# Expert rows by indirect DMA and transposes in place of one-hot products, in a mixture of experts on one Trainium2 core

## The chip, the cores and the metric

The kernel runs on one core of one Trainium2 chip. The time is device microseconds of one execution, from three timed runs; a profiled execution of its own gives the trace. Engines: PE is TensorE's matmuls and PEld its weight loads, DVE is VectorE, ACT is ScalarE, POOL is GpSimd, SP is SyncE, whose queue issues the loads of the weights. A q behind an engine's name (SPq, ACTq) is its sequencer, which issues DMAs.

## The reference, cut to what matters

Two blocks are computed on 512 tokens of width 1024 in float32: a first block (a long convolution and a differential attention) and a second one (sparse attention and a mixture of experts). The change touches the mixture of experts alone:

```python
def hier_moe(h, ...):                       # h: rmsnorm(x) * gain, 512 x 1024
    g_sel = argmax(h @ w_group + b_group)   # one of 4 groups
    top_val, top_idx = top_k(e_logit[g_sel], 2)          # 2 of its 8 experts
    weight = softmax(g_logit)[g_sel] * softmax(top_val)
    # for each of 32 experts, on the rows of its tokens:
    gate, up = split(xb @ w_gate_up[e], 2)               # 1024 -> 2 x 256
    y = (silu(gate) * up) @ w_down[e]                    # 256 -> 1024
    # y * weight is summed into the rows of the tokens
x = x + hier_moe(...); out = rmsnorm(x, norm_final)
```

## The kernel before

All of it is traced into one program for the five engines and then ordered by the framework's own scheduler, which keeps each engine's queue in order; a queue waits at its first instruction that isn't ready.

`moe()` begins while the last projection of the mixer runs. For each of the eight blocks m of 128 columns, `after()` adds up the routing logits `lg`, transposes the block `hn` (columns by tokens) to tokens by columns in PSUM (`tp`), and splits it into a high part `Xh` and a low part `Xl`, both 128 x 4 x 1024, so that two fast matmuls with them keep float32 precision. Then comes the routing, for the 4 x 128 tokens at once: GpSimd raises the mean squares to the power -0.5 (`power`, L1832), VectorE does some 30 small operations one after another (two `first_max` for the best and second expert, weights, ranks) and TensorE a few tiny matmuls. The result is `rk` (the place of each token among those of each expert, up to 64 places per expert), `Wd` (weights) and `wr` (six columns per pair of experts: the weights of the two experts and the token's normaliser, each as a high and a low part). At the end of this stage GpSimd adds `acc = Xh + Xl` (L1902), the array of tokens into which the experts' results are added; `issue_after` puts these four additions behind `power` in GpSimd's queue.

The experts' stage works on 16 pairs of experts j, in 8 groups g of two pairs. `gather(g)` makes a 0/1 matrix `P` (tokens by 4 x 64 places) on VectorE and multiplies `Xh` and `Xl` with it (L1923): for each of eight column blocks kk eight matmuls of 256 columns, an eviction to `Xs` (L1929 on VectorE or L1931 on ScalarE, scaled by the norm's gain). That yields the tokens of four experts, columns by places. After kk = 3 it multiplies `wr` with `P` too (L1937), for the weights `sw` and normalisers `sr` of the places. `gate_up(j)` multiplies `Xs` with the streamed weights of two experts, each on a half of TensorE's columns (L1961), `act(j)` transposes the result (L1970) and applies the gate, `down(j)` multiplies with the second weights (L1984), and `combine(g)` brings the results of two pairs back to the tokens with the matrices `PT` (L2002) and adds them to `acc` (L2005). The loop over j at the end of the stage interleaves these: gate_up(j), down(j-1), then steps of `gather(g+1)` and `combine(g-1)`, then act(j).

The weights, 6 MiB per pair, come in jobs of 1 MiB on SP's queue (`_load`, L220 and L229) into nine buffers taken in turn; a load waits until the matmuls that used its buffer are done. Only in case an expert has more than 64 tokens does `overflow()` do more work behind the end.

Of the kernel before, what the change touches and what calls it, by code (L numbers as in the profile page):

```python
# [20 lines left out]
D = 1024  # L21
KD = D // 128
SEQ = 512
# [6 lines left out]
F32 = np.float32  # L30
# [12 lines left out]
def host_consts():  # L43
    c = {}
    c["ident"] = np.eye(128, dtype=F32)

    t = np.linspace(0.0, 1.0, T, dtype=F32)
    w = (F32(2.0 * math.pi) * np.arange(T, dtype=F32) / F32(T)).astype(F32)
# [3 lines left out]
    n = T // 2 + 1  # L52
# [46 lines left out]
    cm = np.zeros((5, 128, 2, 5, 128), F32)  # L99
# [17 lines left out]
    G = np.zeros((5, 128, 2, 266))  # L117
# [16 lines left out]
    p = np.arange(128) % 64  # L134
    j = (p // 32) * 16 + p % 16
# [6 lines left out]
    pi = np.arange(128)  # L142
# [6 lines left out]
    m = np.zeros((128, 64 + 1 + 128 + 8), F32)  # L149
    m[:, 0:64] = np.arange(64)  # L150
    m[:, 64] = pi % 64
    m[:, 65:193] = pi[:, None] < pi[None, :]
    m[:, 193:201] = pi[:, None] + 128 * np.arange(8)[None, :]
    c["moe"] = m
    return c

# [188 lines left out]
N_PAIR = N_EXP // 2  # L345
# [982 lines left out]
def block2_mixer(k, A, C, out, pp, ppc):  # L1328
    nc, tc = k.nc, k.tc
    RC = slice(META, T)  # L1330
    with ExitStack() as ctx:
# [406 lines left out]
        for m in range(KD):  # L1738
# [11 lines left out]
            ml.append(l)  # L1750
        spc.close()
        moe(k, A, C, out, ctx, mhp, Pairs(mh), Pairs(ml))


def moe(k, A, C, out, ctx, mhp, mh, ml):
    nc, tc = k.nc, k.tc
    rt = ctx.enter_context(tc.tile_pool(name="moer", bufs=1, reuse_waits="tile"))
    acc = rt.tile([128, 4, D], FT, name="acc")
    Xh, Xl = (x.rearrange("p a b -> p (a b)")[:, 0:4 * D].rearrange("p (t d) -> p t d", t=4) for x in (k.xh, k.xl))
    cm = rt.tile([128, 201], FT, name="cm")  # L1760
# [14 lines left out]
    Wd = rt.tile([128, 4, 32], FT, name="Wd")  # L1775
    rs = rt.tile([128, 4], FT, name="rs")
    rkT = rt.tile([32, 512], BF, name="rkT")
    wr = rt.tile([128, 4, N_PAIR, 6], FR, name="wr")
    cnt = rt.tile([128, 32], FT, name="cnt")


    with tc.tile_pool(name="mo1", bufs=2, reuse_waits="tile") as wk, tc.tile_pool(name="mo1x", bufs=1, reuse_waits="tile") as xp, \
# [11 lines left out]
        def after(m, hn, hh, hl, sq):  # L1794
            f, l = m == 0, m == KD - 1
            nc.tensor.matmul(lg[0:36], wrh[:, m], hh, start=f, stop=False)
            nc.tensor.matmul(lg[0:36], wrh[:, m], hl, start=False, stop=False)
            nc.tensor.matmul(lg[0:36], wrl[:, m], hh, start=False, stop=l)
            tp = pp.tile([128, 4, 128], FT, name="tp", bufs=2)
            for i in range(4):  # L1800
                c = slice(i * 128, i * 128 + 128)
                nc.tensor.matmul(st[:, i, m:m + 1], sq[:, c], k.ones, start=True, stop=True)
                nc.tensor.transpose(tp[:, i], hn[:, c], k.ident)
            c = slice(m * 128, m * 128 + 128)
            split(k, tp, Xh[:, :, c], Xl[:, :, c])
        pend = None
        for m in range(KD):
            h2 = wk.tile([128, 512], FT, name="h2", bufs=3)
# [3 lines left out]
            ps = pp.tile([128, 512], FT, name="pg", bufs=2)  # L1812
# [9 lines left out]
            nc.scalar.activation(sq, hn, AF.Square)  # L1822
            pend = (m, hn, hh, hl, sq)
        after(*pend)
        mhp.close()
        rawp = ctx.enter_context(tc.tile_pool(name="moew", bufs=1, reuse_waits="tile", side="right"))
        k.W.more_raw((rawp, N_RAW), (k.W.hl_pool, 4))
# [4 lines left out]
        power = nc.gpsimd.tensor_tensor(rs, rs, k.mhalf.to_broadcast([128, 4]), OP.pow)  # L1832
# [10 lines left out]
        def tiny(n, name):  # L1843
            return xp.tile([128, 4, n], FT, name=name)
# [11 lines left out]
        g, el = L[:, :, 0:4], L[:, :, 4:36]  # L1856
# [26 lines left out]
        d, r = tiny(1, "d"), tiny(1, "r")  # L1883
# [13 lines left out]
        for i in range(4):  # L1897
            nc.tensor.transpose(tr[0:32, i * 128:i * 128 + 128], rk[:, i], k.ident)
        nc.vector.tensor_scalar(rkT, tr[0:32], 100.0, None, op0=OP.min)
        for t in range(4):  # L1900
            with tc.issue_after(power.ins):
                nc.gpsimd.tensor_tensor(acc[:, t], Xh[:, t].bitcast(FT), Xl[:, t].bitcast(FT), OP.add)  # L1902


    NG = N_EXP // 4
    with tc.tile_pool(name="mo2", bufs=2, reuse_waits="tile") as wk, tc.tile_pool(name="mo2y", bufs=1, reuse_waits="tile", side="right") as yp, \
            tc.tile_pool(name="mo2p", bufs=1, reuse_waits="tile", space=PSUM) as pp:
        Xs, SW, PT, Y, G, H = {}, {}, {}, {}, {}, {}

        def gather(g):  # L1910
# [4 lines left out]
            yield  # L1915
            for kk in range(KD):
                if g or kk % 3 == 0:
                    ps = pp.tile([128, 512], FT, name="ga")[:, 0:256]
                else:
                    ps = pp.tile([128, 512], FT, name="gu", bufs=2)[:, 0:256]  # L1920
# [5 lines left out]
                x = wk.tile([128, 4, 64], FT, name="Xs", bufs=16)  # L1926
                v = ps.rearrange("p (e s) -> p e s", e=4)
                if kk % 2:
                    nc.vector.tensor_scalar(x, v, k.gain(5, kk), None, op0=OP.mult)  # L1929
                else:  # L1930
                    nc.scalar.activation(x, v, AF.Copy, scale=k.gain(5, kk))  # L1931
                Xs[g, kk] = x
                if kk == 3:
                    sp = pp.tile([128, 2, 6], FT, name="cb", bufs=2)
                    for j in range(2):
                        for t in range(4):
                            nc.tensor.matmul(sp[:, j], P[:, t, 2 * j:2 * j + 2].rearrange("p e s -> p (e s)"),  # L1937
                                             wr[:, t, 2 * g + j], start=(t == 0), stop=(t == 3))
                    s6 = wk.tile([128, 2, 6], FT, name="s6")
                    nc.vector.tensor_copy(s6, sp)  # L1940
                    s3 = wk.tile([128, 2, 3], FT, name="s3")
                    nc.gpsimd.tensor_tensor(s3, s6[:, :, 0::2], s6[:, :, 1::2], OP.add)
                    w, r = (wk.tile([128, 2], FT, name=n, bufs=3) for n in ("sw", "sr"))
                    for i, a in enumerate((slice(0, 64), slice(64, 128))):
                        nc.gpsimd.tensor_copy(w[a], s3[a, :, i])
                    nc.gpsimd.tensor_copy(r, s3[:, :, 2])
                    SW[g] = (w, r)
                yield

        HALF = (slice(0, 64), slice(64, 128))  # L1950

        def gate_up(j):

            g, i = divmod(j, 2)
            ps = pp.tile([128, 512], FT, name="gu", bufs=2)
            for c in range(2):
                ws = [k.W.get_raw() for _ in HALF]
                for a in range(4):
                    kk = 4 * c + a
                    for x, (o, w) in enumerate(zip(HALF, ws)):  # L1960
                        nc.tensor.matmul(ps[o], Xs[g, kk][:, 2 * i + x], w[:, a], start=(kk == 0), stop=(kk == 7))  # L1961
# [46 lines left out]
        def steps(g, n):  # L2008
            for _ in range(n):
                next(g, None)  # L2010
        for _ in gather(0):
            pass
        nxt = comb = iter(())
        for j in range(N_PAIR):
            g, i = divmod(j, 2)
            if i == 0 and g + 1 < NG:
                nxt = gather(g + 1)
            gate_up(j)
            if j:
                down(j - 1)  # L2020
            if i == 0 and g:
                comb = combine(g - 1)
            steps(nxt, (5, 9)[i])
            steps(comb, 4)
            act(j)
        for _ in comb:
# [156 lines left out]
```

## Time and profile before

| | us |
|---|---|
| median of 3 timed runs (2463.84 to 2469.36) | 2466.86 |
| profiled execution, its own time | 2471.03 |
| its span from the first to the last instruction | 2469.3 |
| routing, TensorE nearly idle | 2083.6 to 2098.3 |
| experts' pairs | 2111.5 to 2440.5 |

Times in the trace count from the span's start. The busy time of an engine in a stretch says how full it is; which of them sets the end is read from the chain of waits, in which each piece of work is listed with the time by which it moved the end. Matmuls overlap, so their durations add up to more than the time they take; the pieces of the chain don't.

### The profile page before, as it was taken

What the parts mean: (1) busy time and instruction counts of PE and PEld (TensorE: products, weight loads), DVE (VectorE), ACT (ScalarE), POOL (GpSimd) and SP (SyncE); (2) the same over time, 40 slices, a digit from 0 to 9 for tenths busy, and PEclk for the clock granted to TensorE, in tenths of its full rate; (3) what the DMA queues carried; (4) which work ended last, traced back from release to release, by engine and by line L of the source; (5) the groups of instructions that cost most, each with busy time, mean ns of one, the idle gap of its engine ahead of it and who ended that gap; (6) DMA issues with size and microseconds to landing.
All of it is one profiled execution on the core that took longest, in us unless ns stands there. A gap on an engine that the chain in (4) does not pass through costs nothing. (4 is left out here: it accounts for less than half of the span.)

```text
span 2469.3 us, 38547 instructions
## 1 busy us (share of the span) xinstructions
PE 2328.6 (94%) x14980; PEld 1946.8 (79%) x14980; DVE 1575.4 (64%) x3032; ACT 1065.7 (43%) x2161; POOL 700.9 (28%) x696
## 2 busy tenths in 40 slices
PE   7999999999999989999999989988999997999997
PEld 6999999998889978888888879876777766554543
DVE  7777764438875696778778544777788664233334
ACT  5666644423344465555555444334444442111111
POOL 3454531125634232323323237321011032000000
PEclk9999999998999899999999999888999998999999
DMA  6333323231145321111112145511221334787873
GB/s 220 120 121 100 113 85 96 86 113 54 54 143 171 130 69 35 60 54 59 53 56 64 52 131 171 166 52 43 77 69 63 120 112 155 265 309 264 319 247 120
DMA packets 266739, 295.79 MB, mean 120 GB/s; under 512 B 20232, under 2 KB 212116, under 8 KB 266170
## 3 DMA queue, kind: packets, MB, share of 16 engines
q1 hardware_dynamic: 228048, 245.90, 30.5%
q10 hardware_dynamic: 35258, 30.54, 4.3%
q0 software_dynamic: 3248, 16.86, 1.8%
q8 instruction: 119, 1.95, 0.3%
q14 instruction: 66, 0.54, 0.1%
HBM read 269.79 MB, written 23.48 MB: 119 GB/s over the span
## 5 line engine op out<-in xcount | busy, mean ns | idle before, releaser
L260 DVE TENSOR_TENSOR wlo<-wraw,whi 128x1024 fp32r<-128x1024 f32 (+2 forms) x201 | 229.0, 1153 | 153.0 <-ACT whi L279 137.6
L260 POOL TENSOR_TENSOR wlo<-wraw,whi 128x1024 fp32r<-128x1024 f32 (+1 forms) x91 | 181.6, 2004 | 502.6 <-ACT whi L279 321.3
L279 ACT CAST whi<-wraw 128x1024 fp32r<-128x1024 f32 x198 | 206.3, 1047 | 182.2 <-PE pj L809 66.9
L807 PE MATMUL ps<-xh,whi 128*128 128x264 f32 x1024 | 215.1, 287 | 5.0 <-ACT hTd L580 4.5
L809 PE MATMUL ps<-xl,whi 128*128 128x264 f32 x1024 | 214.8, 287 | 0.0
L811 PE MATMUL ps<-xh,wlo 128*128 128x264 f32 x1024 | 212.3, 285 | 0.0
L807 PE MATMUL pj<-xh,whi 128*128 128x512 f32 (+2 forms) x544 | 190.9, 356 | 4.3 <-DVE rr L1179 2.9
L809 PE MATMUL pj<-xl,whi 128*128 128x512 f32 (+2 forms) x544 | 188.9, 353 | 0.0
L811 PE MATMUL pj<-xh,wlo 128*128 128x512 f32 (+2 forms) x544 | 188.2, 353 | 0.1
L807 PEld LDWEIGHTS ps<-xh,whi 128*128 128x128 f32 x1024 | 161.4, 190 | 7.2 <-ACT hTd L580 5.3
L809 PEld LDWEIGHTS ps<-xl,whi 128*128 128x128 f32 x1024 | 162.0, 189 | 1.6 <-issue 1.3
L811 PEld LDWEIGHTS ps<-xh,wlo 128*128 128x128 f32 x1024 | 161.4, 190 | 1.2 <-issue 0.8
L809 PE MATMUL pj<-vx,whi 128*128 128x256 f32 (+1 forms) x480 | 137.1, 287 | 0.3 <-DVE vx L326 0.3
L325 ACT CAST pth<-pt 128x512 fp32r<-128x512 f32 (+4 forms) x174 | 84.4, 498 | 113.4 <-PE pt L1636 62.1
L326 DVE TENSOR_TENSOR ptl<-pt,pth 128x512 fp32r<-128x512 f32 (+4 forms) x174 | 97.9, 573 | 50.4 <-ACT pth L325 50.0
L1273 ACT ACTIVATE p<-S,mx 128x528 f32<-128x528 f32 x128 | 89.7, 703 | 78.5 <-DVE mx L1271 60.7
L807 PEld LDWEIGHTS pj<-xh,whi 128*128 128x128 f32 x544 | 103.2, 192 | 19.0 <-DVE rr L1179 3.3
L811 PEld LDWEIGHTS pj<-xh,wlo 128*128 128x128 f32 x544 | 102.6, 192 | 14.2 <-issue 1.0
L809 PEld LDWEIGHTS pj<-xl,whi 128*128 128x128 f32 x544 | 102.8, 191 | 13.1 <-issue 1.0
L1270 DVE TENSOR_REDUCE mx<-S 128x1 f32<-128x528 f32 x128 | 88.7, 701 | 25.6 <-PE S L1269 25.2
L2005 DVE TENSOR_TENSOR acc<-acc,cb 128x512 f32<-128x512 f32 x64 | 43.7, 686 | 84.2 <-PE cb L2002 83.4
L1961 PE MATMUL gu<-wraw,Xs 128*64 128x512 f32 x312 | 93.3, 603 | 0.0
(672 smaller groups left out, 6935.0 us busy)
## 6 DMA issues: line engine op xcount, KB each, us to landing
wraw<-in_w_gate_up_dram SPq DMA_DIRECT2D x39, 1024.0 KB
wraw<-in_hy_w_in_dram SPq DMA_DIRECT2D x32, 1024.0 KB
wraw<-in_da_w_in_dram SPq DMA_DIRECT2D x32, 1024.0 KB
wraw<-in_hy_w_out_dram SPq DMA_DIRECT2D x16, 1024.0 KB
wraw<-in_da_w_out_dram SPq DMA_DIRECT2D x16, 1024.0 KB
wraw<-in_w_down_dram SPq DMA_DIRECT2D x16, 1024.0 KB
whi<-in_w_gate_up_dram SPq DMA_DIRECT2D x25, 512.0 KB
wlo<-in_w_gate_up_dram SPq DMA_DIRECT2D x25, 512.0 KB
```

What stands on the lines that cost most here:

```text
L260: eng.tensor_tensor(l, r, h.bitcast(FT), OP.subtract)
L279: nc.scalar.copy(hf, vf)
L325: nc.scalar.copy(hi, raw)
L326: (lo_eng or nc.vector).tensor_tensor(lo, raw, hi.bitcast(FT), OP.subtract)
L807: nc.tensor.matmul(ps[i], wh[:, kk, fsl], xh[:, kk, c], start=f, stop=False)
L809: nc.tensor.matmul(ps[i], wh[:, kk, fsl], xl[:, kk, c], start=False, stop=False)
L811: nc.tensor.matmul(ps[i], wl[:, kk, fsl], xh[:, kk, c], start=False, stop=l)
L1270: nc.vector.tensor_reduce(mx[:, m:m + 1], S[:, :, 0:TH], AX.XY, OP.max)
L1273: nc.scalar.activation(p.rearrange("p (a b) -> p a b", a=2), S[:, :, 0:TH], AF.Exp, bias=mx[:, m:m + 1], scale=0.125, accum_out=sm[:, m:m ...
L1961: nc.tensor.matmul(ps[o], Xs[g, kk][:, 2 * i + x], w[:, a], start=(kk == 0), stop=(kk == 7))
L2005: nc.vector.tensor_tensor(a, a, ps, OP.add)
```

## The change

The tokens' rows before the norm's gain are now kept as plain float32: `after()` copies each `tp` to `acc` on ScalarE, too, and the four additions on GpSimd are gone. Four DMAs on ScalarE's queue store `acc` to an array `xd` in DRAM, one row of 4 KB per token. `wr` gets two more columns that hold each token's number (constants, appended to the array `cm`), so that the product of `wr` with `P` also gives, for each place, the number of its token.

`prepare(g)` is what is left of `gather(g)`: `P`, the product with `wr` (L1937 before, now eight columns wide and ahead of everything else) and the small copies; for every group but the first it turns the numbers to integers on GpSimd and issues two indirect DMAs from GpSimd, each of which fetches 128 rows (the places of one pair) from `xd` to a tile `xg` (three buffers). `turn(j)` transposes the 128 x 1024 rows of pair j in two blocks of four 128x128 transposes into the one PSUM buffer `ga`, each with four evictions of 128x128 to `Xs`, which is now one tile per pair (two buffers). The first group, experts 0 to 3, still gets its tokens by the products with `Xh` and `Xl` (`first_gather`), with two evictions of 128x128 per column block. In the loop `prepare(g+1)` comes at the start of pair 2g, the first block of `turn(j+1)` behind gate_up(j), the second behind down(j-1).

```diff
@@ after()
             split(k, tp, Xh[:, :, c], Xl[:, :, c])
+            nc.scalar.copy(acc[:, :, c], tp)
@@ behind the projection
         after(*pend)
+        for t in range(4):
+            nc.scalar.dma_start(xd[t * 128:t * 128 + 128], acc[:, t])
@@ end of the routing
-        for t in range(4):
-            with tc.issue_after(power.ins):
-                nc.gpsimd.tensor_tensor(acc[:, t], Xh[:, t].bitcast(FT), Xl[:, t].bitcast(FT), OP.add)
@@ tiles
-    wr = rt.tile([128, 4, N_PAIR, 6], FR, name="wr")
+    wr = rt.tile([128, 4, N_PAIR, 8], FR, name="wr")
+    nc.vector.tensor_copy(wr[:, :, :, 6:8], cm[:, 201:205][:, :, None, None].to_broadcast([128, 4, N_PAIR, 2]))
+    xd = k.dram.tile([SEQ, D], FT, name="xd")
@@ gather(g) becomes
+        def prepare(g):
+            P = ...                                     # as before
+            sp = pp.tile([128, 2, 8], FT, name="cb", bufs=2)
...                                                     # product with wr, as before
+            s8 = wk.tile([128, 2, 8], FT, name="s8")
+            nc.vector.tensor_copy(s8, sp)
+            if g:
+                ix = wk.tile([128, 2], I32, name="ix")
+                nc.gpsimd.tensor_copy(ix, s8[:, :, 6])
+                for j in range(2):
+                    x = XG[2 * g + j] = wk.tile([128, D], FT, name="xg", bufs=3)
+                    nc.gpsimd.indirect_dma_start(out=x, out_offset=None, in_=xd[:, :],
+                                                 in_offset=bass.IndirectOffsetOnAxis(ap=ix[:, j:j + 1], axis=0))
...
+        def scaled(x, v, kk):
+            if kk % 2:
+                nc.vector.tensor_scalar(x, v, k.gain(5, kk), None, op0=OP.mult)
+            else:
+                nc.scalar.activation(x, v, AF.Copy, scale=k.gain(5, kk))
...
+        def turn(j):
+            x = XG.pop(j)
+            Xs[j] = wk.tile([128, KD, 128], FT, name="Xs")
+            for c in range(2):
+                tp = pp.tile([128, 4, 128], FT, name="ga")
+                for a in range(4):
+                    kk = 4 * c + a
+                    nc.tensor.transpose(tp[:, a], x[:, kk * 128:kk * 128 + 128], k.ident)
+                for a in range(4):
+                    scaled(Xs[j][:, 4 * c + a], tp[:, a], 4 * c + a)
+                yield
@@ loop over the pairs
-        for _ in gather(0):
-            pass
-        nxt = comb = iter(())
+        first_gather()
+        comb = iter(())
         for j in range(N_PAIR):
             g, i = divmod(j, 2)
             if i == 0 and g + 1 < NG:
-                nxt = gather(g + 1)
+                prepare(g + 1)
             gate_up(j)
+            nxt = turn(j + 1) if 2 <= j + 1 < N_PAIR else iter(())
+            steps(nxt, 1)
             if j:
                 down(j - 1)
             if i == 0 and g:
                 comb = combine(g - 1)
-            steps(nxt, (5, 9)[i])
+            steps(nxt, 2)
             steps(comb, 4)
             act(j)
```

## Rows read from the trace of the kernel before

**Rows 1.** The page: the span, and the chain that ended last, by engine.

```profile
span 2469.3 us, 38547 instructions
PE 28%; DVE 6%; ACT 1%; issue 1%; ACTq 0%; DMA 0%; POOL 0%; POOLq 0%; DVEq 0%
```

**Rows 2.** Busy time by stage: stretch, length, engines, PEclk, DMA share, GB/s.

```profile
2083.60:2098.30 14.70, 0.41 (x4) 0.39 (x5) 13.49 (x31) 0.73 (x3) 9.95 (x5) 0.55 0.56 213
2098.30:2111.50 13.20, 12.48 (x90) 11.63 (x89) 7.20 (x31) 2.27 (x5) 0.76 (x4) 0.72 0.00 1
2111.50:2440.50 329.00, 328.69 (x1562) 162.75 (x1561) 101.07 (x159) 46.99 (x75) 5.25 (x28) 1.00 0.76 278
```

**Rows 3.** Waits in the experts' stage: who for whom, total us, times, longest.

```profile
SPq L220 <- PE gu L1961: 87.5, 32, 9.4
PEld gu L1961 <- DMA wlo<-in_w_down_dram: 0.5, 2, 0.3
```

**Rows 4.** The chain in the experts' stage: start, us moved, instructions.

```profile
2119.45 1.15 PE ga L1923 x8
2213.41 0.95 PE ga L1923 x8
2252.25 0.44 PE T L1970 x4
2257.43 0.59 PE T L1970 x4
2418.39 1.14 PE ga L1923 x8
```

**Rows 5.** Groups of instructions by form, 2112 to 2440: busy, mean ns, idle before.

```profile
L1931 ACT ACTIVATE Xs<-ga,vc 128x256 f32<-128x256 f32 x28 | 13.3, 475 | 97.6 <-PE ga L1923 97.6
L1963 ACT ACTIVATE G<-gu,sr 128x512 f32<-128x512 f32 x16 | 11.0, 688 | 61.4 <-PE gu L1961 60.6
L1913 DVE TENSOR_TENSOR P<-rk,cm 128x1024 fp32r<-128x1024 f32 x7 | 8.5, 1215 | 0.0
```

**Rows 6.** DMA issues of GpSimd, whole kernel: KB each, median us to landing.

```profile
hdram<-hTd POOLq DMA_DIRECT2D x4, 528.0 KB, 8.3
w<-in_hy_f_w_dram POOLq DMA_DIRECT2D x2, 16.0 KB, 6.5
```

**Rows 7.** Timeline of the routing: start, us, instruction, idle time before it.

```profile
2084.29 9.26 POOL L1902 TENSOR_TENSOR acc<-xh,xl 128x1024 f32<-128x1024 f32 x4
2084.99 1.76 DVE L326 TENSOR_TENSOR wr<-rs,wr 128x64 fp32r<-128x64 f32 x1
2086.86 2.13 DVE L1851 TENSOR_TENSOR ge<-L,gm 128x16 f32<-128x16 f32 x1
2089.02 2.26 DVE L1852 SCALAR_TENSOR_TENSOR ge<-ge,cm 128x16 f32<-128x16 f32 x1
2091.52 2.06 DVE L1854 TENSOR_TENSOR go<-ge,gi 128x16 f32<-128x16 f32 x1
2093.62 0.17 DVE L1859 TENSOR_TENSOR ge<-L,gm 128x16 f32<-128x16 f32 x1
2098.35 0.18 PE L1876 MATMUL rp<-asg,tri 128*128 128x32 bf16 x1 [14.34 <-DVE asg L1871]
```

**Rows 8.** Busy time in a stretch with full DMA engines, columns as in rows 2.

```profile
2160.00:2170.00 10.00, 10.00 (x61) 7.32 (x58) 3.46 (x7) 1.76 (x5) 0.75 (x4) 1.00 1.03 413
```

**Rows 9.** SP's queue: first and last loads of weights in the experts' stage.

```profile
2115.19 0.37 SPq L229 DMA_DIRECT2D wraw<-in_w_down_dram  x1
2429.68 0.88 SPq L229 DMA_DIRECT2D wraw<-in_w_down_dram  x2
```

**Rows 10.** Timeline of ScalarE and its queue before the routing.

```profile
2057.65 0.33 ACTq L1809 DMA_DIRECT2D h<-hdram  x1
2080.99 1.07 ACT L325 CAST xh<-tp 128x512 fp32r<-128x512 f32 x2
2082.94 0.58 ACT L1834 COPY lgs<-lg 36x512 f32<-36x512 f32 x1 [0.88 <-PE lg L1798]
```

More of the change, by code (lines that the diff above doesn't have):

```diff
@@ L147, in host_consts @@
     c["causal"] = np.where(pi[None, :] <= pi[:, None], 0.0, -1e30).astype(F32)
-    m = np.zeros((128, 64 + 1 + 128 + 8), F32)
+    m = np.zeros((128, 64 + 1 + 128 + 8 + 4), F32)
     m[:, 0:64] = np.arange(64)
@@ L153, in host_consts @@
     m[:, 193:201] = pi[:, None] + 128 * np.arange(8)[None, :]
+    m[:, 201:205] = pi[:, None] + 128 * np.arange(4)[None, :]
     c["moe"] = m
@@ L1759, in moe @@
     Xh, Xl = (x.rearrange("p a b -> p (a b)")[:, 0:4 * D].rearrange("p (t d) -> p t d", t=4) for x in (k.xh, k.xl))
-    cm = rt.tile([128, 201], FT, name="cm")
+    cm = rt.tile([128, 205], FT, name="cm")
     nc.scalar.dma_start(cm, C["moe"])
@@ L1831, in moe @@
         nc.vector.tensor_scalar(rs, rs, 1.0 / D, EPS, op0=OP.mult, op1=OP.add)
-        power = nc.gpsimd.tensor_tensor(rs, rs, k.mhalf.to_broadcast([128, 4]), OP.pow)
+        nc.gpsimd.tensor_tensor(rs, rs, k.mhalf.to_broadcast([128, 4]), OP.pow)
         lgs = xp.tile([36, 512], FT, name="lgs")
@@ L1907, in moe @@
             tc.tile_pool(name="mo2p", bufs=1, reuse_waits="tile", space=PSUM) as pp:
-        Xs, SW, PT, Y, G, H = {}, {}, {}, {}, {}, {}
-        def gather(g):
+        Xs, XG, SW, PT, Y, G, H = {}, {}, {}, {}, {}, {}, {}
+        def prepare(g):
             P = wk.tile([128, 4, 4, 64], FR, name="P", bufs=1)
@@ L1914, in gather, with first_gather @@
                                     iota[:, None, None, :].to_broadcast([128, 4, 4, 64]), OP.is_equal)
-            yield
+            sp = pp.tile([128, 2, 8], FT, name="cb", bufs=2)
+            for j in range(2):
+                for t in range(4):
+                    nc.tensor.matmul(sp[:, j], P[:, t, 2 * j:2 * j + 2].rearrange("p e s -> p (e s)"),
+                                     wr[:, t, 2 * g + j], start=(t == 0), stop=(t == 3))
+            s8 = wk.tile([128, 2, 8], FT, name="s8")
[3 more added lines that the diff above has]
+                nc.gpsimd.tensor_copy(ix, s8[:, :, 6])
+                for j in range(2):
+                    x = XG[2 * g + j] = wk.tile([128, D], FT, name="xg", bufs=3)
+                    nc.gpsimd.indirect_dma_start(out=x, out_offset=None, in_=xd[:, :],
+                                                 in_offset=bass.IndirectOffsetOnAxis(ap=ix[:, j:j + 1], axis=0))
+            s3 = wk.tile([128, 2, 3], FT, name="s3")
+            nc.gpsimd.tensor_tensor(s3, s8[:, :, 0:6:2], s8[:, :, 1:6:2], OP.add)
+            w, r = (wk.tile([128, 2], FT, name=n, bufs=3) for n in ("sw", "sr"))
+            for i, a in enumerate((slice(0, 64), slice(64, 128))):
+                nc.gpsimd.tensor_copy(w[a], s3[a, :, i])
+            nc.gpsimd.tensor_copy(r, s3[:, :, 2])
+            SW[g] = (w, r)
+            return P
+        def scaled(x, v, kk):
[3 more added lines that the diff above has]
+                nc.scalar.activation(x, v, AF.Copy, scale=k.gain(5, kk))
+        def first_gather():
+            P = prepare(0)
+            for j in range(2):
+                Xs[j] = wk.tile([128, KD, 128], FT, name="Xs")
             for kk in range(KD):
[L1917 to L1920, printed above, removed]
+                ps = (pp.tile([128, 512], FT, name="gu", bufs=2) if kk % 3 else pp.tile([128, 512], FT, name="ga"))[:, 0:256]
                 for t in range(4):
@@ L1925, in gather @@
                                          stop=(t == 3 and x == 1))
[L1926 to L1947, printed above, removed]
+                for j in range(2):
+                    scaled(Xs[j][:, kk], ps[:, 128 * j:128 * j + 128], kk)
+        def turn(j):
+            x = XG.pop(j)
+            Xs[j] = wk.tile([128, KD, 128], FT, name="Xs")
+            for c in range(2):
[5 more added lines that the diff above has]
+                    scaled(Xs[j][:, 4 * c + a], tp[:, a], 4 * c + a)
                 yield
@@ L1955, in gate_up @@
             ps = pp.tile([128, 512], FT, name="gu", bufs=2)
+            xs = Xs.pop(j)
             for c in range(2):
@@ L1959, in gate_up @@
                     kk = 4 * c + a
-                    for x, (o, w) in enumerate(zip(HALF, ws)):
-                        nc.tensor.matmul(ps[o], Xs[g, kk][:, 2 * i + x], w[:, a], start=(kk == 0), stop=(kk == 7))
+                    for o, w in zip(HALF, ws):
+                        nc.tensor.matmul(ps[o], xs[:, kk, o], w[:, a], start=(kk == 0), stop=(kk == 7))
             G[j] = wk.tile([128, 512], FT, name="G")
```

## The prediction

> **What bounds the kernel now.** The edit lies wholly in the last fifth of the kernel, the mixture of experts, so I read that part alone. The span is 2469.3 us of a profiled run of 2471.0 us; the median of the runs is 2466.9, so the profiled run lies 4.2 above it. TensorE leads the chain that ended last [rows 1]. By stage [rows 2]: from 2083.6 to 2098.3 (the routing) TensorE does almost nothing and VectorE is busy 13.5 of 14.7 us; from 2111.5 to 2440.5 (the expert pairs, "the loop" from here on) TensorE is busy 328.7 of 329.0 us at the full clock while the DMA engines are at 0.76 and VectorE at a third. So the routing is a serial VectorE chain and the loop is TensorE's own work. The waits confirm the loop: weight loads wait for matmuls to release their buffers (87.5 us for that line alone), and matmuls wait for weights only in splinters of 0.3 us [rows 3]. A TensorE microsecond taken out of the loop is therefore worth a microsecond until the transfers become the later ones.
>
> **The change, part by part.**
>
> *Products removed.* Groups 1 to 7 no longer multiply the tokens with a 0/1 matrix: 7 groups x 8 column blocks = 56 blocks of eight matmuls. In the chain a block takes 1.15 us ahead of half-array matmuls and 0.95 us ahead of others [rows 4]; 40 of the 56 stand near the long end. 40 x 1.14 + 16 x 0.97 = 61 us removed (bounds 56 x 0.95 = 53 and 56 x 1.15 = 64).
>
> *Turns added.* Fourteen pairs (2 to 15) get two blocks of four transposes each: 28 blocks. The blocks of act(), four transposes of the same 128x128 f32 form, take 0.44 us ahead of whole-array work and 0.59 ahead of half-array work [rows 4]. 28 x 0.5 = 14 us added (12 to 17). The number of blocks between expert matmuls falls, and with it the changes between half-array and whole-array matmuls; by the difference of 0.15 us between the two ends of act()'s block that is worth 0 to 28 x 0.15 = 4 us more; I take 1. Net on TensorE: 61 - 14 + 1 = 48 us less (36 to 56). The small products for weights and ranks are eight columns wide in place of six: nothing.
>
> *Evictions.* A pair now has eight evictions of 128x128, where a group had eight of 128x256, four a pair. One of 128x256 takes 0.48 us and one of 128x512 takes 0.69 on ScalarE [rows 5], so one of 128x128 is about 0.37: 8 x 0.37 = 3.0 us per pair on two engines where 4 x 0.48 = 1.9 stood. VectorE is busy 101 of the loop's 329 us and ScalarE 47 [rows 2], so this costs nothing as long as the four evictions of a block (0.75 us on two engines) end before the next block of the one "ga" buffer, which down() separates. If that cover were gone: 14 x 0.75 = 10 us. In the first gather the 16 evictions in place of 8 cost 0 to 1 us at its end; I take 0.3.
>
> *Rows by indirect DMA.* Per group: the 0/1 matrix on VectorE (1.2 us, as before [rows 5]), eight small matmuls (less than a block's 1 us), small copies on VectorE and GpSimd, and two indirect DMAs issued from GpSimd, which does 5.25 us of work in the whole loop [rows 2]. No indirect DMA runs in the trace of before. The nearest rows are GpSimd's plain DMAs: a 528 KB store takes 8.3 us from issue to landing, a 16 KB load 6.5 us [rows 6]. A gather here is 128 rows of 4 KB, 512 KiB. From issue to landing I take 8.3 us (6.5 to 17, the upper end for a queue shared with the weights). Its program place gives it a whole pair, some 17 us: the rows of group g+1 are asked for at the start of pair 2g and first turned in pair 2g+1. 1.2 + 1 + 1 (the small copies, by their count an estimate from the 0.17 us of a small VectorE operation in [rows 7]) + 8.3 = 11.5 us against 17: hidden. Behind GpSimd's new instructions only the pair's own small copies are queued.
>
> *Bytes.* 278 GB/s x 329 us = 91.5 MB moved in the loop at a share of 0.76 = 250 us of full engines [rows 2], that is 366 GB/s per full share. Where the engines stay full for 10 us they move 413 GB/s [rows 8]. The gathers add 14 x 0.524 = 7.3 MB, so 98.8 MB: 239 us (at 413) to 270 us (at 366). The loop after is 329 - 48 = 281 us; loading can start only when the first buffer is freed, 3.7 us in, and the last weights are asked for some 11 us before its end [rows 9], which leaves 266 us. So 0 to 4 us if the load were even; for lumps I take 4 us (0 to 12).
>
> The full stretch moves 413 GB/s [rows 8]. Against this stands the Trainium skill, "DMA: Bandwidth & Descriptors", section "Specifications", which puts the limit of HBM for one core at about 358 GB/s. By that rule the bytes would need an estimated 276 us and the loop 291, ten more than TensorE, and the change would trade one limit for another; the trace disagrees, over 10 us at least.
>
> *The sums on GpSimd removed.* After the power of the routing, GpSimd adds Xh + Xl, four times 2.3 us, 9.26 us in all. In just that stretch four small VectorE operations with two operands in SBUF take 1.76, 2.13, 2.26 and 2.06 us, each ending where one of GpSimd's four ends; the same kind of operation right after takes 0.17, on the same 16 columns [rows 7]. They stand in the chain that TensorE waits for (14.34 us, the same group). 8.21 - 4 x 0.18 = 7.5 us less. The granted clock is 0.55 in the idle stretch and 0.72 in the first gather [rows 2], partly the lower level of 1.2 GHz after TensorE stood idle; it will still stand idle for 7 us, and I carry this over at no change.
>
> *Copies and stores added.* Eight copies of 128x512 from PSUM on ScalarE, one per column block. The first six lie beside the projection's matmuls. The last two stand behind the last two casts (1.07 us, ending at 2082.06), and the copy of the logits, for which the logits' transposes and all the routing wait, starts at 2082.94 [rows 10]. Two copies of the same size end at 2083.13, 0.2 us later than that; the four stores take 0.33 us each to issue [rows 10], 1.3 us if they go ahead of the logits. 0 to 1.5 us; I take 0.5, since the order on ScalarE need not put the stores first. The 2 MB stored go out while the weight buffers fill, and the DMA engines stand idle before the loop (1 GB/s from 2098 to 2111 [rows 2]), which covers their 5 us. The ids in wr are one VectorE copy of 128 elements per partition, far from the chain.
>
> *Sum.* 2471.0 - 48 - 7.5 + 0.3 + 0.5 + 4 = 2420.3 in the profiled run's frame, and 4.2 less in that of the median: **2416 us**. The tail from 2440 is the same in both.
>
> **The rivals.**
>
> *A. Transfers set the loop (22%).* Against: 413 GB/s when full [rows 8]. For: 366 on average, and no row shows gathers of 4 KB rows among the weights. With 1.8 us of engine time per gather (8.3 - 6.5 [rows 6]) the demand is 250 + 25 = 275 us, plus the 14.7 us at both ends = 290, nine more than TensorE's 281; with matmuls caught between late weights up to 300. 2416 - 4 + 9..19 = 2421 to 2431; I give 2427. By the 358 GB/s of the Trainium skill, in the same section, it would be an estimated 2422.
>
> *B. Rows come late (11%).* TensorE takes its instructions in order, so a turn placed before its rows have landed holds the weights' matmuls behind it. If landing takes 17 us under the weights' traffic, 3.2 + 17 = 20 us against a pair of 281 / 16 = 17.5: 3 us for the first pair of each group, 21 us in all; if the order puts turns earlier than the program does, twice that. 2437 (2430 to 2455). Against: a lead of a pair, and GpSimd idle.
>
> *C. Slower (4%).* A gather could hold all DMA engines for as long as it takes to land. Weights 250 us + 14 x 8.3 = 366, plus 14.7 = 381 against 329: 52 slower, less the 7.5 of the routing: 2511. It decides from the point where 250 + 14.7 + 14x exceeds 329 + 7, that is x = 5 us per gather. Against: a 16 KB transfer lands after 6.5 us too, so most of 8.3 is latency and not engine time.
>
> *D. The routing gain fails (6%).* If the slow VectorE operations were slow by themselves, 7.5 us stay: 2424. Against: the next operation, behind GpSimd's last sum, takes 0.17 [rows 7].
>
> *E. More than forecast (7%).* TensorE's upper bound 56 and no lumps: 2404.
>
> **How the numbers follow.** The forecast at 2416 (2406 to 2424) has 50%. A to E as above. 2400 to 2440 holds the forecast, A, D, E and the near half of B: over 8 in 10. About 0.2% (5 us) is what a measurement of this kernel can tell from no change. Only C, and a B grown threefold, reach it: faster 0.95, same 0.01, slower 0.04.
>
> **What would show it.** In the profile after: the VectorE operations of the routing at 0.2 us each and TensorE's wait before the ranks' product at about 7 in place of 14.3 us; the loop at about 285 us with TensorE at 97% or more; 28 new blocks of four transposes at 0.44 to 0.59; a DMA share of 0.85 to 0.95. Matmuls of gate_up or down waiting for weights by several us would be A; transposes waiting for a gather, B; gather packets holding the engines for 5 us or more, C. The forecast fails if TensorE's order changes so that its own blocks grow, or if TensorE's waits bring the clock down, which [rows 2] shows after a wait of 14 us and not within the loop.

## The result and the profile after

The changed kernel takes 2428.9 us (median of four runs, 2426.2 to 2429.9), the kernel before 2465.4 us beside it: a ratio of 0.985, 95% interval 0.984 to 0.986. The forecast was 2416 us, in a range of 2400 to 2440: the sign and the range held, the middle was 12.9 us too low. The profiled run lies 2.7 us under the median.

The page of the changed kernel, its span and its chain by engine [rows 1]:

```profile
span 2424.1 us, 38020 instructions
PE 26%; DVE 6%; ACT 2%; issue 1%; ACTq 0%; DMA 0%; POOL 0%; POOLq 0%; DVEq 0%
```

Busy time by stage, for routing, first gather and loop (stretch, length, then PE, PEld, DVE, ACT, POOL, PEclk, DMA share, GB/s) [rows 2]:

```profile
2075.30:2083.30 8.00, 0.47 (x6) 0.45 (x7) 6.23 (x32) 1.36 (x5) 0.94 (x1) 0.60 1.03 378
2083.30:2096.50 13.20, 12.23 (x90) 11.52 (x89) 7.50 (x34) 2.81 (x9) 0.77 (x4) 0.72 0.45 183
2096.65:2401.80 305.15, 293.97 (x1244) 120.55 (x1243) 107.19 (x191) 52.63 (x103) 24.39 (x49) 1.00 0.86 324
```

The routing fell from 14.7 to 8.0 us. In the loop TensorE is no longer busy all the time: 11.2 of 305.2 us are idle, where it was 1.1 of 334.8 to the same mark, the end of the last down product (0.3 of the 329.0 in [rows 2]). What it waits for there (engine, who for whom, us in total, times, longest) came to one wait of 0.3 us, for yh, in the stretch of before up to 2441:

```profile
PE cb L2029 <- ACT yh L2014: 6.7, 6, 1.2
PE T L1997 <- ACT G L1990: 1.8, 2, 0.9
PE cb L2029 <- DVE yl L2015: 1.4, 4, 0.6
PE dn L2011 <- DVE yl L2015: 0.7, 1, 0.7
PE cb L2029 <- DVE acc L2032: 0.5, 1, 0.5
```

None of these is a weight or a fetched row; TensorE's weight loads (PEld) wait for weights in splinters, 2.6 us in all and 0.4 at most. From one mark to the next, in the two profiled runs:

| us | before | after | measured | forecast |
|---|---|---|---|---|
| last logits' product to the loop's first product | 29.0 | 22.2 | -6.8 | -6.7 |
| loop, to the end of the last down product | 334.8 | 305.2 | -29.6 | -44 |
| from there to the end | 22.9 | 22.2 | -0.7 | 0 |

TensorE does the same products ahead of these marks in both kernels. The profiled run of before was 8.1 us later there and is left out: a run of the kernel before with the same code up to that place, further down ("The kernel before in the fixed order"), was 8.7 us earlier than it. So the forecast was right outside the loop, and all that is missing, some 14 us, is missing in it. The first gather takes 13.2 us at a granted clock of 0.72 in both kernels, as the forecast carried it over.

### The profile page after: what moved, and what is told of

It reads as the page before. It is cut to its first block, busy times and chain, and to the rows that moved or that the text cites. A ratio compares the mean times of both kernels' runs of the same rounds, so it can differ in the third digit from the quotient of the medians.

```text
span 2424.1 us, 38020 instructions
## 1 busy us (share of the span) xinstructions
PE 2277.2 (94%) x14644; PEld 1891.3 (78%) x14644; DVE 1574.4 (65%) x3065; ACT 1075.3 (44%) x2201; POOL 709.0 (29%) x713
## 5 line engine op out<-in xcount | busy, mean ns | idle before, releaser
L810 PEld LDWEIGHTS pj<-xl,whi 128*128 128x128 f32 x544 | 102.9, 192 | 13.1 <-issue 1.0
L810 PEld LDWEIGHTS pj<-vx,whi 128*128 128x128 f32 x480 | 90.6, 189 | 1.0 <-DVE vx L327 1.0
```

The costliest lines, as they stand in the source:

```text
L810: nc.tensor.matmul(ps[i], wh[:, kk, fsl], xl[:, kk, c], start=False, stop=False)
```

## The experiments

Two explanations stood at first. Theory 1: the product blocks that were removed had covered the evictions of the down products, and TensorE now waits for these. Rival A of the prediction: the transfers set the pace; its 2427 us is nearly the measured time. Every ratio below is against the kernel before, run beside it on the same chip; that of the change itself is 0.9852. A difference against the change is worked out from the two ratios, times 2465 us.

### The combine one pair later

```diff
-            if i == 0 and g:
+            if i and g:
                 comb = combine(g - 1)
```

> One edit of the changed kernel: the second half of the combine of a group of four experts is begun one pair of experts later, so that TensorE finds only operands whose evictions ended long ago. Nothing else moves. Theory 1 (the loop lost its cover: the combine stands right behind the products whose evictions it reads; in the changed kernel TensorE waits 6.7 us for yh on ScalarE, 1.4 us and 0.7 us for yl on VectorE, 11.2 us idle in the loop in all): the waits for yh and yl vanish, the idle time falls to 3 us or less, the loop goes from 305 us to 294 to 297 us, the total from 2429 us to 2418 to 2421 us. Rival A (the weight transfers set the loop's end): the idle time returns as waits of TensorE for weights, the loop stays within 2 us of 305 us, the total stays at 2427 to 2431 us.

Measured: 2430.6 us, ratio 0.986 (0.984 to 0.988): no gain, as rival A had it. The loop took 308.6 us, with 11.3 us idle. But its trace doesn't show weights. TensorE's waits in the loop:

```profile
PE ga L1971 <- DVE Xs L1944: 4.0, 2, 2.0
PE cb L2029 <- ACT yh L2014: 2.4, 2, 1.2
PE cb L2029 <- DVE acc L2032: 1.8, 2, 1.3
PE T L1997 <- ACT G L1990: 0.9, 1, 0.9
```

The wait for yh fell from 6.7 to 2.4 us, and others came up: the framework's scheduler, given a new place for one block, ordered TensorE's whole queue anew. Twice it put the two blocks of a turn back to back, and the second waited 2.0 us until four evictions, one after another, had emptied the one buffer. Timeline (start, us, engine, line, instruction, idle before):

```profile
2210.64 0.60 PE L1971 MATMUL ga<-ident,xg 128*128 128x128 f32 x4
2211.25 0.42 DVE L2000 SCALAR_TENSOR_TENSOR th<-th,T 128x256 f32<-128x256 f32 x1 [7.29 <-ACT th L1999]
2211.34 0.37 ACT L1946 ACTIVATE Xs<-ga,vc 128x128 f32<-128x128 f32 x1
2211.71 0.42 DVE L2002 SCALAR_TENSOR_TENSOR H<-th,T 128x256 f32<-128x256 f32 x1
2212.05 0.35 DVE L1944 TENSOR_SCALAR Xs<-ga,vc 128x128 f32<-128x128 f32 x1
2212.43 0.37 ACT L1946 ACTIVATE Xs<-ga,vc 128x128 f32<-128x128 f32 x1 [0.72 <-DVE Xs L1944]
2212.83 0.35 DVE L1944 TENSOR_SCALAR Xs<-ga,vc 128x128 f32<-128x128 f32 x1 [0.43 <-ACT Xs L1946]
2213.23 0.93 PE L1971 MATMUL ga<-ident,xg 128*128 128x128 f32 x4 [1.99 <-DVE Xs L1944]
```

### The evictions in two halves

```diff
-            yh, yl = (yp.tile([128, 2, 512], FR, name=n, bufs=4) for n in ("yh", "yl"))
-            nc.scalar.activation(yh, ps, AF.Copy, scale=w)
-            nc.vector.scalar_tensor_tensor(yl, ps, w, ...)
+            yh, yl = ([yp.tile([128, 512], FR, ...) for i in range(2)] for n in ("yh", "yl"))
+            for i in range(2):
+                nc.scalar.activation(yh[i], ps[:, i], AF.Copy, scale=w)
+                nc.vector.scalar_tensor_tensor(yl[i], ps[:, i], w, ...)
...
```

> One edit of the changed kernel: the two evictions of a pair's down products (yh by ScalarE, yl by VectorE, each 128x1024) are each made as two of 128x512 into tiles of their own, so that yl of the first half starts after half of yh, and the first combine product waits for half an eviction. The order of the loop stays. Theory 1 (TensorE waits for these evictions): the waits of the combine for yh fall from 6.7 us to about 3 us, the waits for yl go, the total falls by 4 to 6 us, to 2423 to 2425 us; the two shorter evictions may cost more together than the one (0.1 to 0.2 us a pair), which is covered. Rival A (transfers): within 2 us of 2429 us.

Measured: 2433.8 us, ratio 0.988 (0.986 to 0.990), 6 us above the change. The waits for yh fell to 3.8 us and those for yl to 0.3, as expected, and still the loop took 310.3 us in place of 305.2. The expectation that "the order of the loop stays" was wrong: the combine's blocks stand in 61 places where they stood in 50. So neither run tells theory 1 from rival A: each edit moved the order, too.

### Half the weights

```diff
-                for e in (2 * j, 2 * j + 1):
-                    job(gu[e, h], 0, 512)
+                job(gu[2 * j, h], 0, 512)
...
-                ws = [k.W.get_raw() for _ in HALF]
+                ws = [k.W.get_raw()] * 2
```

> The changed kernel with half the expert weights: each pair loads the weights of its first expert alone and uses them for both halves of the array, so the results of the second experts are other numbers; every product, eviction, combine and gather stays. The loop's load bytes fall from about 91 MB to 46 MB. Theory 1 (the waits for evictions are the loss, not the transfers): the waits for yh and yl stay as they are, 8 to 10 us, only the splinters of waits for weights (2.6 us) go; the total falls by 0 to 5 us, to 2424 to 2429 us. Rival A (the transfers set the pace of the loop): the loop shortens by 10 us or more, the total falls to 2419 us or below.

Measured: 2398.5 us, ratio 0.9742 (0.972 to 0.976), 27 us under the change, and 27 us in the loop: far past theory 1, and what rival A asked for. The loop's row:

```profile
2094.35:2372.15 277.80, 277.18 (x1242) 117.69 (x1241) 107.58 (x191) 52.08 (x103) 24.42 (x49) 1.00 0.50 174
```

Yet the trace of the changed kernel speaks against late weights. Adding up the bytes of SP's packets, less those that the started products had used, the weights lie 3 to 8 MiB ahead of TensorE (the buffers hold 9) until the last loads, never under 3.0. What differed in this run was once more the order, and with it TensorE's idle time: 0.6 us, where theory 1 expected the waits to stay. In the changed kernel the two halves of the array, which can work side by side, go out of step (timeline of TensorE):

```profile
2162.68 0.59 PE L1988 MATMUL gu<-wraw,Xs 128*64 128x512 f32 x1
2162.69 0.59 PE L1988 MATMUL gu<-wlo,Xs 128*64 128x512 f32 x1
2163.11 1.02 PE L1988 MATMUL gu<-whi,Xs 128*64 128x512 f32 x2
2164.06 0.73 PE L2029 MATMUL cb<-yh,PT 128*128 128x512 f32 x2
2164.73 1.50 PE L1988 MATMUL gu<-whi,Xs 128*64 128x512 f32 x5
```

A pair side by side starts at 2162.68 and the next instruction 0.43 us later. At 2163.11 stand two matmuls of one half alone, and they take 0.95 us until 2164.06, as much as two pairs. Counted over the 768 half-array records of the loop (384 matmuls leave two each), 92 start without a partner within 0.1 us in the changed kernel, 84 in the kernel before, 100 and 108 in the two runs above, and 32 in this one. That made theory 2: what half the weights gave was mostly a better order.

### The order fixed

Each of TensorE's instructions in the loop is put behind the one before it in the code, so the scheduler can't move it. (All of them are recorded with one helper's line, L2226.) First with the later combine, then with the combine where the change has it:

```diff
+    def _do(self, f, *a, **kw):          # for te.matmul and te.transpose
...
+            with self.tc.issue_after(self.last):
+                r = f(*a, **kw)
+        self.last = r.ins
...
-                        nc.tensor.matmul(ps[o], xs[:, kk, o], w[:, a], ...)
+                        te.matmul(ps[o], xs[:, kk, o], w[:, a], ...)
```

> The changed kernel with TensorE's order in the loop over the pairs fixed to the order in which the code is written (each matmul is put behind the one before it), and the combine of a group begun one pair later. Operations, bytes and buffers are the same. Theory 2 (the 27 us that half the weights gave back in an earlier run came from the order that the framework's scheduler made with them, not from the transfers: in the changed kernel the weights lie 3 to 8 MiB ahead of TensorE through the whole loop): the two halves of each pair run side by side, TensorE's idle time falls from 11 to 2 us or less, the loop from 305 us to 278 to 284 us, the total from 2429 us to 2402 to 2408 us. Rival A (the transfers set the pace): TensorE waits for weights in the fixed order, the loop stays above 295 us, the total at 2419 us or more.

> The changed kernel with TensorE's order in the loop fixed to the order of the code, and the combine left where the change has it, right behind the down products whose evictions it reads. Against the run with the later combine this is the price of that place alone, in the same order and with the same bytes. Theory 1 (cover of the evictions lost): seven groups wait about 1 us each for yl (1.1 us and 1.3 us of evictions against 1.2 us of other blocks), 5 to 8 us of idle time, the total 5 to 8 us above the run with the later combine. If the evictions are covered: within 2 us of it.

Measured: 2398.6 us, ratio 0.9724 (0.971 to 0.974), and 2402.6 us, ratio 0.9744 (0.972 to 0.977): with the same operations and bytes 32 and 27 us under the change. Records without a partner: 8 and none. Ahead of the loop this order costs 5.0 and 3.0 us (27.2 and 25.2 us from mark to mark, 22.2 in the change): there the small products of `prepare` for the second group stand before the first expert products and wait 1.8 us for the 0/1 matrix. Their rows of the loop, later combine first:

```profile
2104.10:2378.50 274.40, 263.31 (x1233) 119.19 (x1232) 103.91 (x187) 51.32 (x103) 25.36 (x49) 0.99 0.93 360
```

```profile
2100.20:2375.50 275.30, 262.19 (x1233) 117.92 (x1233) 105.11 (x187) 51.46 (x103) 25.46 (x49) 0.99 0.93 359
```

The two misses in it: idle time did not fall to 2 us, and the price of the combine's place came out small. TensorE's waits, later combine first, then the place of the change:

```profile
PE cb L2226 <- DVE acc L2032: 9.0, 13, 0.8
PE gu L2226 <- DMA wraw<-in_w_gate_up_dram: 1.2, 1, 1.2
PE cb L2226 <- DVE yl L2015: 0.8, 1, 0.8
```

```profile
PE cb L2226 <- DVE yl L2015: 6.6, 8, 0.8
PE cb L2226 <- DVE acc L2032: 5.0, 7, 0.8
```

Behind the down products the combine waits for yl, 6.6 us in all (seven of the eight waits, 5.8 us, within the loop), inside the 5 to 8 expected. One pair later it waits for its own two PSUM buffers instead, until VectorE has added them to `acc`. The wait that goes is replaced by the next: 13.1 us idle against 11.1. By the medians the place is worth 4.1 us, less than the two intervals together can tell.

### Half the weights, in the fixed order

> The changed kernel with TensorE's order fixed to the code's, the combine one pair later, and half the expert weights: the weights of each pair's first expert are used for both halves of the array, so the results of the second experts are other numbers. Against the same order with all weights this prices the transfers alone. Theory 2: the same time within 3 us. Rival A: 10 us or more faster than with all weights.

Measured: 2397.1 us, ratio 0.972 (0.969 to 0.974), 1.5 us under the same order with all weights; the loop takes 270.9 us against 274.4. What is gone is for the most part one late load: with all weights TensorE waited once, 1.2 us at 2147.2, and the eight records without a partner stand around it (2145.0 to 2155.4); here there are neither. So of the 27 us by which half the weights shortened the loop, some 3.5 at most are transfers by this pair of runs. And the fixed order alone moves the same bytes in a loop 30 us shorter than the change's. Rival A falls, though its number was the nearest.

### The fetched rows, in the fixed order

```diff
-                    x = XG[2 * g + j] = wk.tile([128, D], FT, name="xg", bufs=3)
-                    nc.gpsimd.indirect_dma_start(out=x, ...)
+                    XG[2 * g + j] = Xh[:, j].bitcast(FT)
```

> The run with TensorE's order fixed and the later combine, without its 14 indirect DMAs: the turns transpose rows that lie in SBUF already, which are other rows than the experts' tokens. All else stays. It prices the fetched rows alone: 7.3 MB among the weights and whatever their landing holds up. If they are hidden as forecast: within 3 us of the same order with the gathers, 2396 to 2401 us. If the gathers hold the DMA engines up or TensorE waits for their rows: 5 us or more faster.

Measured: 2395.4 us, ratio 0.9718 (0.969 to 0.974), against 0.9724 with the gathers, that is 1.5 us, less than the two intervals can tell: hidden, as forecast. The loop takes 270.0 us against 274.4; here, too, that wait and the records without a partner are gone. In this order rivals B and C are out as well.

### The kernel before in the fixed order

> The kernel before with TensorE's order in the loop fixed to the order of the code; nothing else is changed. If the order of the framework's scheduler cost time in the kernel before too (42 of its pairs of half-array matmuls ran one after the other in place of side by side): the loop falls from 335 us to 318 to 328 us, the total from 2465 us to 2448 to 2458 us, and the saving of the change in a fixed order is the 45 us forecast for the loop. If that cost came with the change alone: within 3 us of 2465 us.

Measured: 2465.3 us, ratio 1.000 (0.999 to 1.002): no gain; the loop takes 337.4 us against 334.8. In this order all halves are in step, and TensorE waits elsewhere:

```profile
PE ga L2198 <- ACT Xs L1931: 15.8, 28, 0.6
PE ga L2198 <- DVE Xs L1929: 8.1, 14, 0.6
PE cb L2198 <- DVE acc L2005: 2.4, 5, 0.5
```

The eight product blocks of a gather stand four in a row in the code, in two lots; the second to fourth of each wait for an eviction of the one buffer ga (42 waits in 14 lots). TensorE's idle time is 29.4 us in place of 1.1, about as much as the half-array records save by being in step (167.4 us in place of 194.5, each record taken to last until the next starts). So before, the scheduler's order bought something for its price: it spread the product blocks among the expert products. That with these blocks gone only the price was left is a reading of these numbers, not an experiment. In the fixed order the change is worth 63 us.

This run shows the cover of theory 1, too. In the order of the code the kernel before waits for yh and yl at one place of the loop only, 1.1 us from 2413.9 on, in the last group, which has no gather left to stand between; the changed kernel in that order waits for yl in each of seven groups, 0.8 us every time.

### The sums on GpSimd alone

```diff
+            nc.scalar.copy(acc[:, :, c], tp)
...
-        for t in range(4):
-            with tc.issue_after(power.ins):
-                nc.gpsimd.tensor_tensor(acc[:, t], Xh[:, t].bitcast(FT), Xl[:, t].bitcast(FT), OP.add)
```

> The kernel before with one part of the change alone: the rows that the combine adds to are copied by ScalarE right behind the norm's products, and the four sums by GpSimd are gone. The gather by products stays. Theory of the prediction (VectorE's routing operations of 1.8 to 2.3 us were slow because they ran beside GpSimd's sums of 9.26 us): they take 0.2 us each, routing and first gather together shorten from 29.0 us to 21.5 to 22.5 us, the total falls by 6 to 8 us, from 2465 us to 2457 to 2459 us. Rival D (these operations are slow for another reason, or what they end is not on the path): they stay above 1.5 us, total within 2 us of 2465 us.

Measured: 2457.5 us, ratio 0.998 (0.997 to 0.999); by the ratio 5.4 us (2.2 to 8.6) less. The trace is finer: last logits' product to first product of the loop 29.0 to 21.2 us, with the copies on ScalarE already in it. The operations that took 2.13, 2.26 and 2.06 us [rows 7] (timeline of VectorE):

```profile
2074.62 0.18 DVE L1852 TENSOR_TENSOR ge<-L,gm 128x16 f32<-128x16 f32 x1
2074.83 0.18 DVE L1853 SCALAR_TENSOR_TENSOR ge<-ge,cm 128x16 f32<-128x16 f32 x1
2075.04 0.17 DVE L1854 TENSOR_REDUCE gi<-ge 128x4 f32<-128x16 f32 x1
2075.25 0.17 DVE L1855 TENSOR_TENSOR go<-ge,gi 128x16 f32<-128x16 f32 x1
```

Rival D falls. The Trainium skill, "SBUF — State Buffer", section "Summary: rules for kernel authors", says that when a VectorE operation with two inputs in SBUF meets a GpSimd operation that reads SBUF, the one issued second is held until the first has finished; the two traces agree (2.1 to 2.3 us beside the sums, 0.17 to 0.18 without them).

### Loads shared by both halves

Why the scheduler lets the halves go out of step was tried once. Each load now brings half the depth for both experts of a pair:

```diff
-                for e in (2 * j, 2 * j + 1):
-                    job(gu[e, h], 0, 512)
+                jobs.append((2, [(gu[e, h], 0, 512) for e in (2 * j, 2 * j + 1)], None))
...
```

> The changed kernel with the scheduler free to order, and one thing about the weights changed: each 1 MiB load holds half as much depth for both experts of a pair, in place of twice the depth for one expert, so that the two halves of the array always get their weights from the same load. Bytes, buffers, products and the places in the code stay. Theory 3 (the scheduler lets the two halves go out of step because it expects their weights in different loads; in the changed kernel 92 of 768 half-array matmuls ran without a partner): fewer than 40 run alone, the loop falls from 305 us to 285 to 296 us, the total from 2429 us to 2409 to 2420 us. If the halves go out of step for another reason: 80 or more alone, total within 4 us of 2429 us.

Measured: 2448.0 us, ratio 0.9926 (0.991 to 0.994): 18 us slower than the change, 132 records without a partner, the loop at 321.6 us; 5 of the 18 us stand ahead of the loop (27.4 us from mark to mark). Theory 3 falls, and the "within 4 us" of its rival is missed as well. The reason for the scheduler's order stays open. Half the weights brought the count from 92 to 32, so the bytes that it expects may have a part in it; that run also gave both halves one load, which by this run doesn't do it alone.

### The blocks spread

On the fixed order with the later combine, the combine's four blocks per pair stand two ahead of the down products and two behind, and `prepare` stands behind gate_up; at the end, what is left of the last but one combine is split around the last down products:

```diff
+            gate_up(j)
             if i == 0 and g + 1 < NG:
                 prepare(g + 1)
-            gate_up(j)
             steps(nxt, 1)
+            steps(comb, 2)
             if j:
                 down(j - 1)
...
-            steps(comb, 4)
+            steps(comb, 2)
             act(j)
+        steps(comb, 3)
+        down(N_PAIR - 1)
         for _ in comb:
             pass
-        down(N_PAIR - 1)
```

> The changed kernel with TensorE's order in the loop fixed, as in the run with the later combine, and two places moved in the code: the combine's four blocks per pair are given as two before the down products and two behind them, so that its two PSUM buffers are read out under other blocks (in the run before TensorE waited 9.0 us in all, 13 times up to 0.8 us, for the sums that free them), and the small products for weights and ranks come behind the pair's first products (there they held the start of the loop up by 1.8 us for the 0/1 matrix). Theory 2, that the loop is TensorE's own order and what it waits for: the waits for these sums fall to 2 us or less, the loop from 274 us to 264 to 268 us, the routing and first gather from 27 us to 22 to 24 us, the total from 2399 us to 2384 to 2391 us. If the transfers set a floor near 270 us: waits for weights of 5 us or more appear and the total stays at 2394 us or more.

Measured: 2383.5 us, ratio 0.9669 (0.966 to 0.968), 45 us under the change and the fastest of all. The loop's row, TensorE's waits, and the DMA packets from 2150 to 2350 us:

```profile
2100.80:2361.90 261.10, 257.90 (x1229) 118.33 (x1228) 100.76 (x187) 51.97 (x103) 25.45 (x49) 0.99 0.97 378
PE ga L2228 <- DMA xg<-xd,ix: 2.9, 1, 2.9
PE cb L2228 <- DVE acc L2032: 1.0, 2, 0.7
DMA packets 33382, 81.00 MB, mean 405 GB/s; under 512 B 1835, under 2 KB 1835, under 8 KB 33370
```

The waits for the sums fell from 9.0 to 1.0 us, and the stretch ahead of the loop is back at 22.2 us. The loop came out 3 us under the 264 to 268 expected. The 2.9 us is rival B in small: the first group's rows are asked for later and come late, once. Now the transfers are nearly as full as TensorE, at a share of 0.97, and from 2150 us on the weights lie 2.4 to 4.4 MiB ahead; no matmul waits for weights (two weight loads do, 0.4 and 0.3 us).

## Why the prediction was right, and where it was not

*Routing: right.* -7.5 + 0.3 + 0.5 = -6.7 us forecast, -6.8 measured. The sums gone and the copies added gave 29.0 - 21.2 = 7.8 in a run of their own, so the stores, the sixteen evictions and the rest cost 22.2 - 21.2 = 1.0, where 0.8 was set with the copies in it. On ScalarE one of the two last copies went ahead of the logits, and the stores went behind them:

```profile
2074.27 0.59 ACT L1810 COPY acc<-tp 128x512 f32<-128x512 f32 x1 [0.27 <-DVE xl L327]
2074.88 0.58 ACT L1841 COPY lgs<-lg 36x512 f32<-36x512 f32 x1
2075.97 2.00 ACTq L1831 DMA_DIRECT2D xd<-acc  x4
```

*Products and turns: right.* From the starts of all of TensorE's records in the loop, each lasting until the next: products 61.2 us (61 forecast), turns 15.7 (14), of which 0.9 is waiting.

*"Costs nothing as long as the four evictions end": the step that failed.* It was asked of the turns' own buffer ga and of no other. What the product blocks had covered was the evictions of the down products. In the code the combine of a group follows the down products that it reads; before, four product blocks stood between, now one block of transposes, and here the scheduler put even that behind:

```profile
2213.02 0.59 PE L2011 MATMUL dn<-wraw,H 128*64 128x512 f32 x1
2213.65 1.11 ACT L2014 ACTIVATE yh<-dn,sw 128x1024 fp32r<-128x1024 f32 x1 [3.20 <-PE dn L2011]
2214.80 1.28 DVE L2015 SCALAR_TENSOR_TENSOR yl<-dn,sw,yh 128x1024 fp32r<-128x1024 f32 x1 [3.44 <-ACT yh L2014]
2214.81 0.73 PE L2029 MATMUL cb<-yh,PT 128*128 128x512 f32 x2 [1.20 <-ACT yh L2014]
2215.38 0.60 PE L1971 MATMUL ga<-ident,xg 128*128 128x128 f32 x4
```

TensorE's idle time went from 1.1 to 11.2 us over the loop, 10 of the 14 missing; 8.8 of the 11.2 are waits for yh and yl. In the order of the code the waits for yl stand in every group with the change, and before it only where no product block is left. That these waits alone could be taken out was not shown: each run that removed them moved the order or met the next wait. The turns' cover was mis-sized, too: the four evictions of a block go in turn, ScalarE and VectorE waiting for each other (21.1 and 24.2 us in the changed kernel's loop), so a block takes 1.8 us from the first's start to the end of the last in the timeline of the later combine, part of it behind another VectorE operation, not 0.75 on two engines; in the changed kernel's order it stayed covered.

*"The number of blocks between expert matmuls falls": wrong.* 56 product blocks went, but the runs of half-array matmuls went from 78 to 72 only, and the combine's blocks stand in 50 places where they stood in 45; in the fixed order the runs are 31. Without idle time, TensorE's records other than products and turns take 6.7 us more than before, where 1 us less was forecast. With the idle time (10.1), the turns (0.9 over, without waiting) and the 4 us of lumps that did not come: 10.1 + 6.7 + 1 + 0.9 - 4 = 14.7, about the 14 missing. The halves out of step are hardly part of it: all half-array records together take 195.7 us, against 194.5 before, where 84 had no partner. Why the blocks were cut up this way stays open. The sum took TensorE's other blocks as they were; the clause "if TensorE's order changes so that its own blocks grow" stood there without a price.

*Transfers: the lumps of 4 us were not there.* That is luck: without this term the forecast would have been 2412 us, 17 us too low in place of 13. 91.2 + 7.3 = 98.6 MB in the loop (98.8 forecast). A gather took 7.9 us to land (8.3 forecast) and no transpose waited for one:

```profile
q1 hardware_dynamic: 38592, 91.23, 79.2%
q0 software_dynamic: 2016, 7.34, 6.4%
xg<-xd,ix POOLq DMA_INDIRECT x14, 7.9
```

*The 281 us of the loop: reached, but not by this kernel.* To the mark of the table, the end of the last down product, these 281 us are 334.8 - 48 = 287. The fixed order takes 275.3 us, idle time of 13.1 included. It gets under the forecast because it also puts the halves in step (all half-array records 171.3 us), a price that the kernel before had paid and the forecast carried over. The work taken out and put in was estimated well; that the rest of TensorE's order would stay as it was, was assumed.

The rivals: A gave 2427 us, 2 us from the result, by a mechanism that the runs in the fixed order refute: the same bytes in a loop 30 us shorter, and about 2 us each by the ratios for half the weights and for no gathers. B, C and D didn't happen.

## What to carry to other kernels

Before a block is costed at its own length, list every eviction that runs while it does, not only that of its own buffer; and check that the order that was built around the block still makes sense without it. Where a scheduler orders the queue, one edit is an edit of the order as well, and experiments tell causes apart only once the order is held fixed. A rival that gives the right time is not yet the right cause.

## What the hardware showed that was not expected

A 128x64 matmul of 512 columns without a partner on the other half holds TensorE for as long as a pair side by side (0.43 us to the next start in both cases), so each pair out of step costs a whole step more.

The transfers held 405 GB/s over 200 us with gathers among them, in the last run. The forecast's 413 was from 10 us; the Trainium skill's limit of some 358 GB/s ("DMA: Bandwidth & Descriptors", section "Specifications") doesn't show here, and at that rate the loop's 98.6 MB would have needed an estimated 275 us where the loop took 261.1.
